# Relu and row mean on one core: tiles of 16 rows in 3 buffers instead of 8 rows in 6, and a last tile loaded in halving pieces

## The chip, the core and the metric

The kernel runs on one core of a Trainium2 chip. The metric is device time in microseconds (us), the median of several runs; lower is better. The engines that do work here are VectorE (DVE in the profile), ScalarE (ACT), and SyncE (SP), whose queue only issues transfers (DMAs). 16 DMA engines carry the transfers between the chip's main memory and the core's own memory. The core's own memory has 128 partitions, and a tile is a block of columns on all of them.

## The reference

```python
def setup_inputs():
    batch, seq, dim = 32, 512, 1024
    return {"x": np.random.randn(batch, seq, dim).astype(np.float32)}

def reference(x):
    relu_x = np.maximum(x, 0)
    return np.mean(relu_x, axis=-1).astype(np.float32)
```

Every one of the 16384 rows of 1024 floats is clipped at zero and averaged. 67.1 MB are read and 64 KB are written; there is one clip and one addition for each number.

## The kernel before, in words

The 16384 rows are dealt to the partitions: partition p holds the 128 neighbouring rows 128p to 128p+127, so that its input is one stretch of 512 KB. Below, "a row" is one row on every partition: 128 x 1024 floats, 512 KB.

The work goes over 16 tiles. A tile is 8 rows, which is 32 KB on each partition and 4 MB in all, and is loaded by one DMA from SP's queue (line 36). The pool named `in` has 6 buffers, so the first six loads are issued at once, and each later load waits on SP until the tile that had its buffer has been worked through.

The rows of a tile are shared out one by one. ScalarE takes the even rows (line 40): an activation with Relu, in place, whose accumulator gives the sum of the row. VectorE takes the odd rows (line 47): a maximum with zero, in place, again with an accumulator. Each accumulator is stored by a short instruction of its own behind the main one, which the profile lists as a READ_ACCUMULATOR. The sums go into one column for each row: `res_s` from ScalarE, `res_v` from VectorE.

Behind the last tile, line 56 (VectorE) scales the odd columns of `res_v` by 1/1024 into `res_s`, line 57 (ScalarE) scales the even columns of `res_s`, and line 58 stores `res_s`, 512 bytes on each partition, from SP's queue.

A framework sets the waits between the engines from what each instruction reads and writes. In the listings of the order, a wait such as DMAHW3 is a wait for the landing of a transfer (eight such counters are used in turn), DVE and Activation are waits for VectorE's and ScalarE's earlier work. Each engine runs its instructions in program order.

Of the kernel before, what the change touches and what calls it, by code (L numbers as in the profile page):

```python
# [1 line left out]

# [4 lines left out]


@with_exitstack  # L10
def kernel(
    ctx: ExitStack,
    tc: tile.TileContext,
    x: bass.AP,
    out: bass.AP,
):
    nc = tc.nc
    P = nc.NUM_PARTITIONS
    xf = x.flatten_outer_dims()
    R, D = xf.shape  # L20
    assert R % P == 0
    J = R // P
    xr = xf.rearrange("(p j) d -> p j d", p=P, j=J)
    outr = out.flatten().rearrange("(p j) -> p j", p=P, j=J)

    nb = 8
    assert J % nb == 0
    ntiles = J // nb

    with tc.tile_pool(name="in", bufs=6) as pool, tc.tile_pool(name="res", bufs=1) as rpool:  # L30
        res_s = rpool.tile([P, J], mybir.dt.float32)
        res_v = rpool.tile([P, J], mybir.dt.float32)
        for t in range(ntiles):
            j0 = t * nb
            xt = pool.tile([P, nb, D], mybir.dt.float32)
            nc.sync.dma_start(out=xt, in_=xr[:, j0:j0 + nb, :])  # L36
            for n in range(nb):
                j = j0 + n
                if j % 2 == 0:
                    nc.scalar.activation(  # L40
                        out=xt[:, n, :],
                        in_=xt[:, n, :],
                        func=mybir.ActivationFunctionType.Relu,
                        accum_out=res_s[:, j:j + 1],
                    )
                else:
                    nc.vector.tensor_scalar(  # L47
                        out=xt[:, n, :],
                        in0=xt[:, n, :],
                        scalar1=0.0,  # L50
                        scalar2=None,
                        op0=mybir.AluOpType.max,
                        op1=mybir.AluOpType.add,
                        accum_out=res_v[:, j:j + 1],
                    )
        nc.vector.tensor_scalar_mul(out=res_s[:, 1::2], in0=res_v[:, 1::2], scalar1=1.0 / D)  # L56
        nc.scalar.mul(out=res_s[:, 0::2], in_=res_s[:, 0::2], mul=1.0 / D)  # L57
        nc.sync.dma_start(out=outr, in_=res_s)


# [1 line left out]
_INS = ['x']  # L62
_OUTS = [((32, 512), 'float32')]


# [23 lines left out]
```

## Time and profile before

| what | value |
|---|---|
| time, median of 3 runs | 169.04 us (168.8 to 169.05) |
| span of the profiled execution, first to last instruction | 166.8 us |
| time outside the span, against that median | 2.2 us |
| VectorE busy | 74.5 us, 45% of the span |
| ScalarE busy | 69.8 us, 42% of the span |
| main memory read, mean over the span | 67.11 MB, 403 GB/s with the store |
| first and last tile, VectorE starts on it | 13.40 us and 159.42 us |
| store of the result issued | 164.37 us |

The span runs from the first to the last instruction on the core. The profiled execution has no separate device time of its own on record; the timed runs are 2.2 us above its span, which is what lies ahead of the first instruction and behind the last. "Busy" counts the time in which an engine runs instructions; waits are listed apart with the thing that ended them. The DMA share is the mean over the 16 DMA engines. A window counts a transfer's packet, with all its bytes and its whole duration, in the window in which it starts.

### The profile page before, as it was taken

How to read it: one execution, taken by the hardware profiler on the slowest of the kernel's cores; microseconds unless marked ns; L12 is line 12 of the kernel's file. 1: busy time of each engine (PE TensorE's matmuls, PEld its weight loads, DVE VectorE, ACT ScalarE, POOL GpSimd, SP SyncE). 2: the span in 40 equal slices, each digit the busy share in tenths (PEclk: the TensorE clock that was granted, in tenths of full speed). 3: DMA queues.
4: the chain of work that ended last, by engine and by line, in shares of the span. 5: the costliest groups of instructions: out<-in, count | busy, mean ns of one | idle time of the engine just before them, and what ended most of it. 6: DMA issues, size and time to landing. Idle time of an engine off the chain costs nothing.

```text
span 166.8 us, 353 instructions
## 1 busy us (share of the span) xinstructions
DVE 74.5 (45%) x129; ACT 69.8 (42%) x130; POOL 0.2 (0%) x4
## 2 busy tenths in 40 slices
DVE  0007346190734619073460907347090734609073
ACT  3007245180724518072450907246090724519073
POOL 0000000000000000000000000000000000000000
DMA  6999999999999999999999999999999999999700
GB/s 228 401 448 432 440 432 432 440 401 448 424 448 424 440 432 409 456 409 448 432 420 432 440 440 409 448 424 432 432 440 432 424 440 417 440 432 432 338 0 16
DMA packets 2450, 67.19 MB, mean 403 GB/s; under 512 B 272, under 2 KB 400, under 8 KB 400
## 3 DMA queue, kind: packets, MB, share of 16 engines
q1 hardware_dynamic: 2448, 67.18, 93.9%
q14 instruction: 2, 0.02, 0.0%
HBM read 67.11 MB, written 0.07 MB: 403 GB/s over the span
## 4 chain that ended last, share of the span: by engine, by line
DVE 34%; another core or an unknown queue 33%; DMA 29%; SPq 1%; issue 1%; DVEq 0%
DVE xt L47 33%; DMA xt<-in_x_dram 29%; SPq L36 1%; DVEq L47 0%; DVE res_s L56 0%
## 5 line engine op out<-in xcount | busy, mean ns | idle before, releaser
L47 DVE TENSOR_SCALAR_CACHE_REDUCE xt<-xt 128x1024 f32<-128x1024 f32 x64 | 74.2, 1216 | 89.7 <-DMA xt<-in_x_dram 89.7
L40 ACT ACTIVATE xt<-xt 128x1024 f32<-128x1024 f32 x64 | 66.8, 1044 | 93.4 <-DMA xt<-in_x_dram 93.4
L40 ACT ACTIVATION_READ_ACCUMULATOR xt<-xt 128x1 f32 x64 | 11.9, 187 | 0.0
L47 DVE DVE_READ_ACCUMULATOR xt<-xt 128x1 f32 x64 | 5.3, 83 | 0.0
L40 ACT ACT_TABLE_LOAD x1 | 1.3, 1283 | 0.7 <-PEq L73 0.7
L57 ACT ACTIVATE res_s<-res_s 128x64 f32<-128x64 f32 x1 | 0.3, 263 | 0.0
L56 DVE TENSOR_SCALAR res_s<-res_v 128x64 f32<-128x64 f32 x1 | 0.2, 196 | 0.0
L73 POOL MEMSET const-uint8-127<- 128x1 uint8 x1 | 0.1, 102 | 0.0
L73 POOL MEMSET const-bfloat16-1.0<- 128x1 bf16 x1 | 0.1, 101 | 0.0
L73 POOL MEMSET const-float32-0.0<- 128x1 f32 x1 | 0.1, 98 | 0.2 <-issue 0.2
L73 POOL MEMSET const-float32-1.0<- 128x1 f32 x1 | 0.1, 98 | 0.0
## 6 DMA issues: line engine op xcount, KB each, us to landing
xt<-in_x_dram SPq DMA_DIRECT2D x16, 4096.0 KB, 53.5
out_dram<-res_s SPq DMA_DIRECT2D x1, 64.0 KB, 1.6
```

The source lines that it names most:

```text
L36: nc.sync.dma_start(out=xt, in_=xr[:, j0:j0 + nb, :])
L40: nc.scalar.activation(out=xt[:, n, :], in_=xt[:, n, :], func=mybir.ActivationFunctionType.Relu, accum_out=res_s[:, j:j + 1],)
L47: nc.vector.tensor_scalar(out=xt[:, n, :], in0=xt[:, n, :], scalar1=0.0, scalar2=None, op0=mybir.AluOpType.max, op1=mybir.AluOpType.add, a ...
L56: nc.vector.tensor_scalar_mul(out=res_s[:, 1::2], in0=res_v[:, 1::2], scalar1=1.0 / D)
L57: nc.scalar.mul(out=res_s[:, 0::2], in_=res_s[:, 0::2], mul=1.0 / D)
L73: nc = _bacc.Bacc("TRN2", target_bir_lowering=False, num_devices=1)
```

## The change

The tile is 16 rows: 64 KB on each partition, 8 MB in all, in 3 buffers, so the memory for input stays the same. Seven such tiles are loaded whole. The eighth is loaded by seven DMAs into one buffer: 8, 4, 2 and 1 rows, and then the last row in columns of 512, 256 and 256. The rows are shared out as before up to row 13 of that tile. Row 14 is halved: ScalarE sums its first 512 columns, VectorE the rest, and VectorE adds the two. Of the last row, ScalarE sums the first 256 columns, VectorE the other three quarters one by one, with a small instruction that adds what is there before the last quarter. The means of the first 112 rows are written ahead of the last tile (`finish(0, j0)`), those of the next 14 ahead of row 14. The results now go to a tile `res` of their own.

```diff
-    nb = 8
-    assert J % nb == 0
-    ntiles = J // nb
+    NB = 16
+    BUFS = 3
+    full = J // NB - 1
 
-    with tc.tile_pool(name="in", bufs=6) as pool, tc.tile_pool(name="res", bufs=1) as rpool:
-        for t in range(ntiles):
-            j0 = t * nb
-            xt = pool.tile([P, nb, D], mybir.dt.float32)
-            nc.sync.dma_start(out=xt, in_=xr[:, j0:j0 + nb, :])
...
-        nc.vector.tensor_scalar_mul(out=res_s[:, 1::2], in0=res_v[:, 1::2], scalar1=1.0 / D)
-        nc.scalar.mul(out=res_s[:, 0::2], in_=res_s[:, 0::2], mul=1.0 / D)
-        nc.sync.dma_start(out=outr, in_=res_s)
+    row_pieces = []
+    left = NB
+    while left > 1:
+        row_pieces.append(left // 2)
+        left -= left // 2
+    col_pieces = [D // 2, D // 4, D // 4]
...
+    def rows(xt, lo, n, j0):
+        for k in range(lo, lo + n):
+            j = j0 + k
+            if j % 2:
+                dve_row(nc, xt[:, k, :], sum_v[:, j:j + 1])
+            else:
+                act_row(nc, xt[:, k, :], sum_a[:, j:j + 1])
+
+    def finish(lo, hi):
+        nc.vector.tensor_scalar_mul(out=res[:, lo + 1:hi:2], in0=sum_v[:, lo + 1:hi:2], scalar1=inv)
+        nc.scalar.mul(out=res[:, lo:hi:2], in_=sum_a[:, lo:hi:2], mul=inv)
+
+    for t in range(full):
+        j0 = t * NB
+        xt = in_pool.tile([P, NB, D], F32, name="xt")
+        nc.sync.dma_start(out=xt, in_=xr[:, j0:j0 + NB, :])
+        rows(xt, 0, NB, j0)
+
+    j0 = full * NB
+    xt = in_pool.tile([P, NB, D], F32, name="xt")
+    lo = 0
+    for n in row_pieces:
+        nc.sync.dma_start(out=xt[:, lo:lo + n, :], in_=xr[:, j0 + lo:j0 + lo + n, :])
+        lo += n
+    c = 0
+    for w in col_pieces:
+        nc.sync.dma_start(out=xt[:, lo, c:c + w], in_=xr[:, j0 + lo, c:c + w])
+        c += w
+
+    finish(0, j0)
+    lo = 0
+    for n in row_pieces[:-1]:
+        rows(xt, lo, n, j0)
+        lo += n
+    finish(j0, j0 + lo)
+
+    last = xt[:, NB - 1, :]
+    act_row(nc, xt[:, lo, :D // 2], part_a[:, 0:1])
+    dve_row(nc, xt[:, lo, D // 2:], part_v[:, 0:1])
+    act_row(nc, last[:, :D // 4], part_a[:, 1:2])
+    dve_row(nc, last[:, D // 4:D // 2], part_v[:, 1:2])
+    nc.vector.tensor_scalar(
+        out=res[:, J - 2:J - 1], in0=part_a[:, 0:1], scalar1=part_v[:, 0:1], scalar2=inv,
+        op0=ALU.add, op1=ALU.mult,
+    )
+    dve_row(nc, last[:, D // 2:3 * D // 4], part_v[:, 2:3])
+    nc.vector.tensor_scalar(
+        out=part_v[:, 1:2], in0=part_v[:, 1:2], scalar1=part_a[:, 1:2], scalar2=part_v[:, 2:3],
+        op0=ALU.add, op1=ALU.add,
+    )
+    dve_row(nc, last[:, 3 * D // 4:], part_v[:, 3:4])
+    nc.vector.tensor_scalar(
+        out=res[:, J - 1:J], in0=part_v[:, 3:4], scalar1=part_v[:, 1:2], scalar2=inv,
+        op0=ALU.add, op1=ALU.mult,
+    )
+    nc.sync.dma_start(out=outr, in_=res)
```

`act_row` and `dve_row` are the two instructions of before (an activation with Relu and an accumulator, a maximum with zero and an accumulator), now in functions: line 15 and line 20 of the changed kernel.

On SP's queue, the last five transfers of before, each but the store a whole tile:

```order
L36 DMA xt<-in_x_dram 128x8192 [waits DMAHW6_49,DVE_49,Activation_49]
L36 DMA xt<-in_x_dram 128x8192 [waits DMAHW7_49,DVE_49,Activation_49]
L36 DMA xt<-in_x_dram 128x8192 [waits DMAHW0_49,DVE_49,Activation_49]
L36 DMA xt<-in_x_dram 128x8192 [waits DMAHW1_49,DVE_49,Activation_49]
L58 DMA out_dram<-res_s 128x128 [waits DVE_49,Activation_49]
```

And SP's queue in the changed kernel, from the last whole tile on:

```order
L79 DMA xt<-in_x_dram 128x16384 [waits DMAHW3_49,DVE_49,Activation_49]
L86 DMA xt<-in_x_dram 128x8192 [waits DMAHW4_49,DVE_49,Activation_49]
L86 DMA xt<-in_x_dram 128x4096
L86 DMA xt<-in_x_dram 128x2048
L86 DMA xt<-in_x_dram 128x1024
L90 DMA xt<-in_x_dram 128x512
L90 DMA xt<-in_x_dram 128x256
L90 DMA xt<-in_x_dram 128x256 [waits DMAHW5_49]
L120 DMA out_dram<-res 128x128 [waits DMAHW6_49,DVE_49,Activation_49]
```

The last 8 MB come in seven transfers instead of two. The first piece waits for the buffer of the fifth whole tile, the five behind it wait for nothing, and the last one waits for the landing of the sixth whole tile.

On VectorE, the end of the program before: the last two tiles of four odd rows each, and the scaling.

```order
L47 TENSOR_SCALAR xt,res_v<-xt 128x1024 [waits DMAHW6_49,DVE_49,Activation_49]
L47 TENSOR_SCALAR xt,res_v<-xt 128x1024 x3
L47 TENSOR_SCALAR xt,res_v<-xt 128x1024 [waits DMAHW7_49,DVE_49,Activation_49]
L47 TENSOR_SCALAR xt,res_v<-xt 128x1024 x3
L56 TENSOR_SCALAR res_s<-res_v 128x64 [waits DVE_49]
```

And the end of VectorE's program in the changed kernel, from the piece of four rows on (`part_a` and `part_v` hold the partial sums of the last two rows):

```order
L20 TENSOR_SCALAR xt,sum_v<-xt 128x1024 [waits DMAHW0_49]
L20 TENSOR_SCALAR xt,sum_v<-xt 128x1024
L20 TENSOR_SCALAR xt,sum_v<-xt 128x1024 [waits DMAHW1_49]
L73 TENSOR_SCALAR res<-sum_v 128x7 [waits DVE_49]
L20 TENSOR_SCALAR xt,part_v<-xt 128x512 [waits DMAHW2_49]
L106 TENSOR_SCALAR res<-part_a,part_v 128x1 [waits DVE_49,Activation_49]
L20 TENSOR_SCALAR xt,part_v<-xt 128x256 [waits DMAHW3_49]
L20 TENSOR_SCALAR xt,part_v<-xt 128x256 [waits DMAHW4_49]
L111 TENSOR_SCALAR part_v<-part_v,part_a 128x1 [waits DVE_49,Activation_49]
L20 TENSOR_SCALAR xt,part_v<-xt 128x256 [waits DMAHW5_49]
L116 TENSOR_SCALAR res<-part_v 128x1 [waits DVE_49]
```

Behind the landing of the last transfer stand one row of 256 columns and one instruction of one column, where four rows and one instruction of 64 columns stood. The addition for row 14 (line 106) comes ahead of the first column piece of the last row, though it stands behind it in the code.

More of the change, by code (lines that the diff above doesn't have):

```diff
@@ L7, with act_row, dve_row @@
 from concourse._compat import with_exitstack
+F32 = mybir.dt.float32
+ALU = mybir.AluOpType
+RELU = mybir.ActivationFunctionType.Relu
+def act_row(nc, src, acc):
+    nc.scalar.activation(out=src, in_=src, func=RELU, accum_out=acc)
+def dve_row(nc, src, acc):
+    nc.vector.tensor_scalar(
+        out=src, in0=src, scalar1=0.0, scalar2=None,
+        op0=ALU.max, op1=ALU.add, accum_out=acc,
+    )
 @with_exitstack
@@ L22 @@
     J = R // P
+    inv = 1.0 / D
     xr = xf.rearrange("(p j) d -> p j d", p=P, j=J)
     outr = out.flatten().rearrange("(p j) -> p j", p=P, j=J)
-    nb = 8
-    assert J % nb == 0
-    ntiles = J // nb
-    with tc.tile_pool(name="in", bufs=6) as pool, tc.tile_pool(name="res", bufs=1) as rpool:
-        res_s = rpool.tile([P, J], mybir.dt.float32)
-        res_v = rpool.tile([P, J], mybir.dt.float32)
-        for t in range(ntiles):
-            j0 = t * nb
-            xt = pool.tile([P, nb, D], mybir.dt.float32)
[L36 to L58, printed above, removed]
@@ new lines @@
+    NB = 16
[7 more added lines that the diff above has]
+    col_pieces = [D // 2, D // 4, D // 4]
+    in_pool = ctx.enter_context(tc.tile_pool(name="in", bufs=BUFS))
+    res_pool = ctx.enter_context(tc.tile_pool(name="res", bufs=1))
+    sum_a = res_pool.tile([P, J], F32)
+    sum_v = res_pool.tile([P, J], F32)
+    res = res_pool.tile([P, J], F32)
+    part_a = res_pool.tile([P, 2], F32)
@@ new lines @@
+    part_v = res_pool.tile([P, 4], F32)
+    def rows(xt, lo, n, j0):
[13 more added lines that the diff above has]
+        rows(xt, 0, NB, j0)
@@ L62 @@
+    dve_row(nc, last[:, 3 * D // 4:], part_v[:, 3:4])
+    nc.vector.tensor_scalar(
+        out=res[:, J - 1:J], in0=part_v[:, 3:4], scalar1=part_v[:, 1:2], scalar2=inv,
+        op0=ALU.add, op1=ALU.mult,
+    )
+    nc.sync.dma_start(out=outr, in_=res)
 _INS = ['x']
```

## The prediction

> **What bounds the kernel now.** I read the page first (busy shares, DMA line, costliest groups), then the waits, then windows one tile long, then the timeline of the end. The page:
>
> ```profile
> span 166.8 us, 353 instructions
> DVE 74.5 (45%) x129; ACT 69.8 (42%) x130; POOL 0.2 (0%) x4
> DMA  6999999999999999999999999999999999999700
> ...
> DMA packets 2450, 67.19 MB, mean 403 GB/s; under 512 B 272, under 2 KB 400, under 8 KB 400
> ...
> L47 DVE TENSOR_SCALAR_CACHE_REDUCE xt<-xt 128x1024 f32<-128x1024 f32 x64 | 74.2, 1216 | 89.7 <-DMA xt<-in_x_dram 89.7
> L40 ACT ACTIVATE xt<-xt 128x1024 f32<-128x1024 f32 x64 | 66.8, 1044 | 93.4 <-DMA xt<-in_x_dram 93.4
> L40 ACT ACTIVATION_READ_ACCUMULATOR xt<-xt 128x1 f32 x64 | 11.9, 187 | 0.0
> L47 DVE DVE_READ_ACCUMULATOR xt<-xt 128x1 f32 x64 | 5.3, 83 | 0.0
> ...
> L57 ACT ACTIVATE res_s<-res_s 128x64 f32<-128x64 f32 x1 | 0.3, 263 | 0.0
> L56 DVE TENSOR_SCALAR res_s<-res_v 128x64 f32<-128x64 f32 x1 | 0.2, 196 | 0.0
> ...
> xt<-in_x_dram SPq DMA_DIRECT2D x16, 4096.0 KB, 53.5
> out_dram<-res_s SPq DMA_DIRECT2D x1, 64.0 KB, 1.6
> ```
>
> Neither engine is half busy, and all that they wait for is the input. The DMA engines are full until two or three slices before the end. Tile by tile (columns: window, length, VectorE, ScalarE, GpSimd, clock, DMA share, GB/s):
>
> ```profile
> 61.97:71.81 9.84, 4.65 (x9) 4.31 (x9) 0.00 (x0) 1.00 1.00 433
> 71.81:81.51 9.70, 4.64 (x9) 4.26 (x9) 0.00 (x0) 1.00 1.01 432
> 81.51:91.45 9.94, 4.64 (x9) 4.26 (x9) 0.00 (x0) 1.00 1.00 430
> 130.30:140.02 9.72, 4.65 (x9) 4.27 (x9) 0.00 (x0) 1.00 1.00 432
> 140.02:149.74 9.72, 4.66 (x9) 4.28 (x9) 0.00 (x0) 1.00 1.00 432
> ```
>
> A tile lands every 9.7 us and takes 4.65 us of work. The DMA share is 1.00 across the joint from one transfer to the next: 4.19 MB / 9.71 us is 432 GB/s, the rate inside the window, so nothing is lost at a joint. So the stream sets the time until its last byte, and the end is what VectorE does behind it:
>
> ```profile
> 13.40 1.22 DVE L47 TENSOR_SCALAR_CACHE_REDUCE xt<-xt 128x1024 f32<-128x1024 f32 x1 [13.40 <-DMA xt<-in_x_dram]
> ...
> 149.72 1.22 DVE L47 TENSOR_SCALAR_CACHE_REDUCE xt<-xt 128x1024 f32<-128x1024 f32 x1 [5.07 <-DMA xt<-in_x_dram]
> ...
> 159.38 1.06 ACT L40 ACTIVATE xt<-xt 128x1024 f32<-128x1024 f32 x1 [5.44 <-DMA xt<-in_x_dram]
> 159.42 1.22 DVE L47 TENSOR_SCALAR_CACHE_REDUCE xt<-xt 128x1024 f32<-128x1024 f32 x1 [5.06 <-DMA xt<-in_x_dram]
> 160.57 0.08 DVE L47 DVE_READ_ACCUMULATOR xt<-xt 128x1 f32 x1
> 160.57 1.22 DVE L47 TENSOR_SCALAR_CACHE_REDUCE xt<-xt 128x1024 f32<-128x1024 f32 x1
> ...
> 163.99 0.08 DVE L47 DVE_READ_ACCUMULATOR xt<-xt 128x1 f32 x1
> 164.10 0.20 DVE L56 TENSOR_SCALAR res_s<-res_v 128x64 f32<-128x64 f32 x1
> ```
>
> The last tile is seen at 159.42 and VectorE ends at 164.30: 4.88 us of tail. A row starts 1.15 us after the one ahead of it, and lasts 1.22 with its accumulator read. From 164.30 to the span's end are 2.5 us for the store, which the change leaves as it is:
>
> ```profile
> 164.37 0.35 SPq L58 DMA_DIRECT2D out_dram<-res_s  x1
> ```
>
> **The change, part by part.** *Buffers.* A tile of 16 rows lands every 19.4 us (twice 9.7) and needs about 9.2 us of VectorE (8 rows by 1.14, and 0.08). The fourth load is issued when the first tile has been worked through, near 32.3 (8 rows land at 13.40, 16 at 13.40 + 9.7 = 23.1, and 9.2 behind that), when two loads of 8 MB are still under way until 23.1 + 38.8 = 61.9: 29 us to spare, and the same for each load behind it. SP's waits now:
>
> ```profile
> SPq L36 <- DVE xt L47: 98.3, 10, 14.0
> ```
>
> SP already waits 98.3 us in ten waits with nothing lost at the joints; all that stands behind such a wait on SP are later loads. The six added issues (0.35 us by the store's row, 0.4 by the first loads) lie near 110 us, when the sixth and seventh tile are queued. The last piece also waits for the sixth tile, which lands near 120, almost 40 us before that piece is due. Cost of all this: nothing; cover: the queued loads. Without the cover a late issue would cost its own lateness.
>
> *Packets.* No row shows a packet over 32 KB. In the full windows above a DMA engine moves 432/16 = 27.0 GB/s, so a packet of 32 KB takes 1.214 us. The smallest data packets are the store's 128 of 512 bytes, and they come with 16 of a few bytes for the counter:
>
> ```profile
> 164.90:165.90 1.00, 0.00 (x0) 0.00 (x0) 0.00 (x0) 1.00 0.23 66
> 157.50:158.00 0.50, 0.00 (x0) 0.00 (x0) 0.00 (x0) 1.00 0.16 66
> ```
>
> 0.23 x 1 us x 16 / 128 = 28.8 ns for each. A line through both gives, as an estimate, 9.9 ns for a packet and 36.8 ns for a KB. The page's 2450 packets are 16 tiles x 128 of 32 KB, the 128 of the store, and small ones, so a DMA engine moves 128 of 32 KB; the change has 7 x 8 of 64 KB and 7 x 8 in the pieces, 112: 16 x 9.9 ns = 0.16 us less. Bounds: a gain of 0.55 us if 64 KB packets save their half (56 x 9.9 ns) and the pieces pay nothing more; for the loss there is no row. A 64 KB packet slower by p costs 56p, and the whole gain below is gone at p = 64 ns, 2.6% of 2.43 us. I take 0.1 us of gain, as the rate of 432 holds at 32 KB and the packets cost only by their count in these two rows.
>
> *The tail.* With the joints free, the piece of 8 rows ends where the tile before last does now, at 149.72, and 9.70/8 = 1.21 us pass for a row. So VectorE can see: 4 rows at 154.57, 2 rows at 157.00, row 14 at 158.21, the columns at 158.82, 159.12 and 159.42. Durations by the line through 1216 ns (1024 columns) and 196 ns (64): 1.0625 ns a column, so 672 ns for 512, 400 for 256, 135 for 7, 130 for one. An instruction that waits for VectorE's own last result starts 0.03 later (163.99 + 0.08 to 164.10). VectorE's chain:
>
> The last whole tile lands where a window ends above, at 140.02, is done at 149.2, and its scaling (56 columns, 0.19) lies at 149.4: in time. 4 odd rows end at 154.36, 2 at 156.93, each just ahead of the next piece. Row 13: 157.00 to 158.22. Scaling of 7: to 158.39. Half of row 14: 158.41 to 159.08. Its addition: to 159.24. First columns: 159.25 to 159.65. Second: start 0.08 ahead of that end, as the rows do, to 159.97. Addition: to 160.13. Last columns: to 160.54. Last addition: to **160.70**.
>
> So the last columns are there at 159.42 and VectorE comes to them at 160.14. The landing is hidden by the chain from row 13 on, with 0.7 us to spare; a landing-bound end would be 159.42 + 0.40 + 0.16 = 159.98. ScalarE is a near tie: 8 x 1.04 a tile keeps it ahead; row 12 from 156.96 (it starts 0.04 ahead of VectorE) to 158.11, scaling of 7 (0.22) to 158.36, half of row 14 (1044 − 512 x 0.81 = 628 ns, and 0.09 of read) to 159.10, when VectorE asks for it at 159.11. If it comes later, the chain moves by as much. The addends with a wait are bounded by 83 ns (accumulator read) and 196 ns (64 columns), so the three additions by −0.14 and +0.20 us together. And a wait for a DMA costs VectorE a little of its own, as the chain of waits has it for the last tile:
>
> ```profile
> 159.28 0.03 issue
> 159.31 0.05 DVEq L47
> 159.36 0.06 issue
> 159.42 4.66 DVE xt L47 x8
> ```
>
> The landing times above hold this 0.14 where VectorE waits. At the four waits behind which it finds the data there, I put 0.03 each, and 0.1 in all; the bounds are nothing and 4 x 0.14 = 0.56.
>
> The Trainium skill ("VectorE: DVE Perf Modes", on the extra latency of SBUF-source instructions) has a fixed cost of about 150 cycles in each instruction, 156 ns, where my line has 128 to 130. By the page the tail would end 0.17 us later; no run here has yet shown a row of 256 columns.
>
> *Sum.* 164.30 − 160.70 = 3.60 us less of tail, 0.1 less of stream, and 0.1 against it for the added waits: the span goes from 166.8 to 163.2. The 2.2 us outside it stay. Against the median of 169.04, which I take for this execution's own time, that is **165.4 us**, 2.1% faster.
>
> **The rivals.**
>
> *A: the landing sets the end, and comes earlier.* Packets of 64 KB gain 0.55, the two windows of 9.84 and 9.94 lose their excess of 0.35, and the small instructions are at their low bound. For it: those two windows. Against it: the chain on VectorE from row 13 on is as long as before, and only what moves row 13 counts. Time: 165.4 − 0.55 − 0.14 = 164.7; with the 0.35, 164.4.
>
> *B: the small column pieces come in late.* The store of 64 KB needs 1.6 us from issue to landing, though its packets are moved in a part of that. If each of the three column pieces (256, 128, 128 KB) took 1.6 us behind the one ahead, the last would be seen at 158.21 + 4.8 = 163.01, and VectorE would end at 163.57: 2.87 us later, 168.3 us. Against it: the joints at full share. In between, up to 0.7 us of lateness costs nothing, since VectorE comes at 160.14.
>
> *C, slower than before: each piece pays for its start and its landing in line.* All six added joints cost 1.6 us: the last columns are seen at 159.42 + 9.6 = 169.0, VectorE ends at 169.6, 5.3 us later than now: 174.3 us. It decides from (164.30 − 0.56 − 159.42)/6 = 0.72 us a joint. For it: the 1.6 us. Against it: fifteen joints of 4 MB transfers without a gap, and the pieces are queued 40 us ahead. The Trainium skill ("DMA: Bandwidth & Descriptors", under the anatomy of one DMA and the measured bandwidths) gives some 2.0 us fixed for each DMA and asks for 1 MiB or more in each. Taken in line at its figure, the last landing is 12 us later and the time 176.7 us; the windows above speak against taking it in line.
>
> *D: 64 KB packets are cut in two, or are slower.* Cut in two, the packets are those of before and the forecast stands within 0.5 us. Slower by 64 ns each, the time is 169.0; nothing in the rows shows that, and nothing shows the opposite.
>
> **How the numbers follow.** Forecast 0.70, its own range 164.9 to 166.0 (the bounds on the additions, the waits, the ScalarE tie). A 0.12, B 0.09, C 0.04, D at or above the old time 0.05. The range takes in A and the near part of B (half a microsecond past the cover): 164.4 to 166.4. A measurement of this kernel can tell about 0.2%, 0.34 us, from no change. Faster: 0.70 + 0.12 + 0.08 of B = 0.90; the same: 0.01 of B and 0.03 of D; slower: 0.04 + 0.02.
>
> **What would show it.** Windows of 19.4 us at 432 GB/s show packets and buffers right; a window above 19.9 shows D. VectorE's start on row 13 near 157.0 shows the joints free. On the last columns VectorE should show no wait for a DMA, and start near 160.1; idle time there for a DMA of over 0.3 us shows B. A wait of the addition of row 14 for ScalarE shows the tie lost. VectorE's end should be near 160.7 and the span near 163.2. A span over 165 makes the prediction wrong, and then the landing times of the pieces say which step fell.

## The result, and the profile after

The changed kernel takes 164.86 us (median of 4 runs, 164.74 to 164.88) beside 168.95 us before (4 runs, 168.80 to 169.05): a ratio of 0.9765, 95% interval 0.9751 to 0.9779, 2.3% faster. The forecast was 165.4 us in a range of 164.4 to 166.4. The span of the profiled execution went from 166.8 to 163.1 us, where the prediction had 163.2.

The page of the changed kernel:

```profile
span 163.1 us, 351 instructions
DVE 75.4 (46%) x139; ACT 69.4 (43%) x133; POOL 0.2 (0%) x4
...
DMA packets 2162, 67.19 MB, mean 412 GB/s; under 512 B 240, under 2 KB 624, under 8 KB 880
...
L20 DVE TENSOR_SCALAR_CACHE_REDUCE xt<-xt 128x1024 f32<-128x1024 f32 (+1 forms) x67 | 74.4, 1172 | 84.9 <-DMA xt<-in_x_dram 84.8
```

Both engines are as busy as before, and still wait only for the input. The packets fell from 2450 to 2162 (896 for the whole tiles, 896 for the pieces, 128 of the store and 242 small ones), so the 16 rows do come as one packet of 64 KB on each partition: rival D's first half (packets cut in two) is out. Windows of the change, each between VectorE's starts on two whole tiles that follow one another (window, length, VectorE, ScalarE, GpSimd, clock, DMA share, GB/s):

```profile
42.50:61.90 19.40, 9.21 (x17) 8.43 (x17) 0.00 (x0) 1.00 1.00 432
61.90:81.40 19.50, 9.23 (x17) 8.48 (x17) 0.00 (x0) 1.00 0.99 430
100.90:120.30 19.40, 9.22 (x17) 8.47 (x17) 0.00 (x0) 1.00 1.00 432
```

The stream is full, with 9.2 us of work under each 19.4 us of loading. The timeline of the end, VectorE and what it meets (start, duration):

```profile
149.32 1.22 DVE L20 TENSOR_SCALAR_CACHE_REDUCE xt<-xt 128x1024 f32<-128x1024 f32 x1 [0.24 <-DMA xt<-in_x_dram]
...
156.62 1.22 DVE L20 TENSOR_SCALAR_CACHE_REDUCE xt<-xt 128x1024 f32<-128x1024 f32 x1
...
157.88 0.17 DVE L73 TENSOR_SCALAR res<-sum_v 128x7 f32<-128x7 f32 x1
157.91 0.63 ACT L15 ACTIVATE xt<-xt 128x512 f32<-128x512 f32 x1
157.96 0.68 DVE L20 TENSOR_SCALAR_CACHE_REDUCE xt<-xt 128x512 f32<-128x512 f32 x1
...
158.75 0.21 DVE L106 TENSOR_SCALAR res<-part_a,part_v 128x1 f32<-128x1 f32 x1
...
158.88 0.41 DVE L20 TENSOR_SCALAR_CACHE_REDUCE xt<-xt 128x256 f32<-128x256 f32 x1
...
159.22 0.42 DVE L20 TENSOR_SCALAR_CACHE_REDUCE xt<-xt 128x256 f32<-128x256 f32 x1
...
159.75 0.27 DVE L111 TENSOR_SCALAR part_v<-part_v,part_a 128x1 f32<-128x1 f32 x1
159.94 0.41 DVE L20 TENSOR_SCALAR_CACHE_REDUCE xt<-xt 128x256 f32<-128x256 f32 x1
...
160.39 0.21 DVE L116 TENSOR_SCALAR res<-part_v 128x1 f32<-128x1 f32 x1
```

Row 13 starts at 156.62, where the prediction had 157.00. VectorE never waits for a DMA behind it (no bracket behind the rows), and ends at 160.60, where the prediction had 160.70. So from row 13 on VectorE needs 3.98 us, not 3.70. By the counters in the trace, the piece with row 13 landed at 156.59, row 14 at 157.89, and the columns at 158.5, 158.9 and 159.2. VectorE comes to the last columns at 159.94, 0.75 us behind their landing.

### The profile page after: what moved, and what is told of

Same layout as the page of the kernel before. It is cut to its first block, busy times and chain, and to the rows that moved or that the text cites. A ratio compares the mean times of both kernels' runs of the same rounds, so it can differ in the third digit from the quotient of the medians.

```text
span 163.1 us, 351 instructions
## 1 busy us (share of the span) xinstructions
DVE 75.4 (46%) x139; ACT 69.4 (43%) x133; POOL 0.2 (0%) x4
## 2 busy tenths in 40 slices
DMA packets 2162, 67.19 MB, mean 412 GB/s; under 512 B 240, under 2 KB 624, under 8 KB 880
## 4 chain that ended last, share of the span: by engine, by line
DMA 83%; DVE 14%; SPq 1%; issue 0%; DVEq 0%
DMA xt<-in_x_dram 83%; DVE xt L20 13%; SPq L86 0%; SPq L79 0%; DVE part_v L111 0%; DVE res L116 0%; DVE res L106 0%; DVE res L73 0%; DVEq L20 0%; DVEq L111 0%; DVEq L106 0%
## 5 line engine op out<-in xcount | busy, mean ns | idle before, releaser
L20 DVE TENSOR_SCALAR_CACHE_REDUCE xt<-xt 128x1024 f32<-128x1024 f32 (+1 forms) x67 | 74.4, 1172 | 84.9 <-DMA xt<-in_x_dram 84.8
L15 ACT ACTIVATE xt<-xt 128x1024 f32<-128x1024 f32 (+1 forms) x65 | 66.7, 1027 | 88.9 <-DMA xt<-in_x_dram 88.9
L74 ACT ACTIVATE res<-sum_a 128x56 f32<-128x56 f32 (+1 forms) x2 | 0.5, 232 | 0.1
```

The costliest lines, as they stand in the source:

```text
L15: nc.scalar.activation(out=src, in_=src, func=RELU, accum_out=acc)
L20: nc.vector.tensor_scalar(out=src, in0=src, scalar1=0.0, scalar2=None, op0=ALU.max, op1=ALU.add, accum_out=acc,)
L74: nc.scalar.mul(out=res[:, lo:hi:2], in_=sum_a[:, lo:hi:2], mul=inv)
```

## The experiments

Each kernel was timed beside the kernel before on one chip, whose median there was 168.78, 168.82 and 168.80 us in the three groups (1 to 4, 5 to 8, 9 to 12). The theory was: the stream moves 67.1 MB at a rate that only its packet count changes; VectorE's chain from row 13 on, and not the last landing, sets the end.

One thing that no edit was meant to change moves the end by up to 0.2 us. In every profile the store lands 1.54 to 1.57 us behind its issue. But the last work of SyncE is to check the counters of the transfers one after another, some 0.06 us apart, and the store's counter is one of them. Which one it is follows from the number of loads, since the eight counters are used in turn. The checks from the store's own counter on come behind its landing, so they lengthen the span:

| checks behind the store's landing | kernels, with their loads | landing to the span's end, us |
|---|---|---|
| 2 | before (16) | 0.85 |
| 3 | the change and experiments 3, 7, 8, 11, 12 (14), 2 (9) | 0.88 to 0.92 |
| 4 | 1 (21), 6 (13) | 0.94, 0.96 |
| 5 | 4 (36), 5 and 10 (12) | 1.00, 1.01 |
| 6 | 9 (11) | 1.06 |

None of the expectations below knew of it. Where two kernels differ in it, 0.06 us for each check is taken off before their times are read.

### 1. The tail alone, on tiles of 8 rows

```diff
-    NB = 16
-    BUFS = 3
+    NB = 8
+    BUFS = 6
```

> The tail of the change on tiles of 8 rows (32 KB a partition) in 6 buffers: 15 whole tiles, then 4, 2, 1 rows and the three column pieces. Against the change, 120 packets of 32 KB and 48 smaller ones on a DMA engine instead of 56 of 64 KB and 56 smaller: 56 more. Theory (a packet costs about 9 ns whatever its size, and the larger packets brought the stream forward by it): 56 x 9 ns = 0.5 us more than the change, 165.35 us. Rival (the packet size does nothing, the stream's 0.4 us came from elsewhere in the change, for instance from the fewer waits of SP): 164.9 us.

Measured: 165.57 us (165.49 to 165.78), ratio 0.9808 (0.9796 to 0.9821). The mark on the same chip is experiment 3, which is as fast as the change: 165.01. So tiles of 8 rows cost 0.56 us, of which 0.06 is one more check, and the rival is out. VectorE's row 13:

```profile
157.17 1.22 DVE L20 TENSOR_SCALAR_CACHE_REDUCE xt<-xt 128x1024 f32<-128x1024 f32 x1
```

It is 0.55 later than in the change (and 0.49 later than in experiment 3, where it starts at 156.68), and 0.50 us by 56 packets is 8.9 ns a packet (with the counters of seven more transfers in it). The tail is worth 168.78 − 165.57 = 3.2 us by itself.

### 2. The large tiles alone

```diff
-    row_pieces = []
-    left = NB
-    while left > 1:
-        row_pieces.append(left // 2)
-        left -= left // 2
-    col_pieces = [D // 2, D // 4, D // 4]
+    row_pieces = [8, 8]
...
-    finish(0, j0)
...
+    rows(xt, 0, NB, j0)
+    finish(0, J)
```

> Tiles of 16 rows in 3 buffers, the last one loaded as 8 + 8 rows, with the end of the kernel before (four odd rows and the scaling behind the last landing). Theory (packets bring 0.4 us, the halving pieces all the rest): 168.5 us, VectorE's start on the last 8 rows near 159.0 and its end near 163.9 us in the span. Rival (large tiles alone bring nothing): 168.95 us. A second rival (large tiles cost, and the pieces pay for it): over 169.2 us.

Measured: 168.38 us (12 runs, 168.05 to 169.00), ratio 0.9975 (0.9966 to 0.9985): 0.40 us less, as the theory has it, and 0.46 without the one check more. The timeline of the last tile:

```profile
159.15 1.22 DVE L20 TENSOR_SCALAR_CACHE_REDUCE xt<-xt 128x1024 f32<-128x1024 f32 x1 [4.94 <-DMA xt<-in_x_dram]
...
163.82 0.20 DVE L66 TENSOR_SCALAR res<-sum_v 128x64 f32<-128x64 f32 x1
```

The start was 159.42 before, 0.27 later in this pair of executions, and the 4.87 us behind it are those of before. Not all of the 0.27 is the stream's. The tile before landed at 159.28 and VectorE started 0.14 behind that, since its first row waits for three counters (the order listing of before), two of them in an instruction of its own ahead of the row. Here the piece landed at 159.12 and the row, which has one wait, started 0.02 behind. Without these 0.12 the times leave 0.34 us for the packets, 6 ns for each of 56 fewer.

The two halves of the change, 0.4 and 3.2 us, add up to 3.6 of the 3.8 us that experiment 3 shows for both on this chip.

### 3. Two buffers

```diff
-    BUFS = 3
+    BUFS = 2
```

> The change with 2 buffers instead of 3. Theory (a load is needed in the queue only while the one ahead runs, and it is issued 9.2 us after a landing with 19.4 us of the next tile to go, so 10 us early): no change, 164.9 us within 0.2. Rival (the queue has to hold two waiting loads, or the deeper queue hides something at the joint): 165.9 us or more, with windows of 19.4 us below 430 GB/s.

Measured: 165.01 us (164.93 to 165.12), ratio 0.9774 (0.9761 to 0.9786). The change repeated on other chips gave 164.99 and 164.89: no difference, as the theory has it. SP's waits, and the last whole tile:

```profile
SPq L79 <- DVE xt L20: 107.1, 5, 30.8
```

```profile
139.69 1.22 DVE L20 TENSOR_SCALAR_CACHE_REDUCE xt<-xt 128x1024 f32<-128x1024 f32 x1 [10.15 <-DMA xt<-in_x_dram]
```

SP waits 107.1 us for buffers where the change waits 87.4, and the tile still lands within 0.05 us of the change's 139.64. The third buffer is not needed.

### 4. Tiles of 4 rows

```diff
-    NB = 16
-    BUFS = 3
+    NB = 4
+    BUFS = 12
```

> The tail of the change on tiles of 4 rows (16 KB a partition) in 12 buffers: 31 whole tiles, then 2, 1 rows and the column pieces, 248 + 40 packets on a DMA engine, 176 more than in the change. Theory (9 ns a packet): 1.6 us more than the change, 166.45 us. Rival (32 KB is past a knee below which packets cost much more, or joints of smaller transfers cost): 167.5 us or more. Other rival (packet size does nothing): 164.9 us.

Measured: 166.68 us (166.64 to 166.69), ratio 0.9872 (0.9859 to 0.9884): 1.67 us over experiment 3, 1.55 without the two checks more, for 176 packets: 8.8 ns each with the counters of 22 more transfers. A window of the full stream, and row 13:

```profile
80.00:100.00 20.00, 9.47 (x16) 8.76 (x16) 0.00 (x0) 1.00 1.01 428
```

```profile
158.30 1.21 DVE L20 TENSOR_SCALAR_CACHE_REDUCE xt<-xt 128x1024 f32<-128x1024 f32 x1
```

The DMA engines stay full and only the rate falls, to 428 GB/s. There is no knee from 64 KB down to 16 KB a packet, just the count. The packets themselves say the same. In the trace of the change there are packets of every size from 512 bytes (the store) to 64 KB, each twice the one below, and their median durations are 27, 46, 84, 159, 309, 611, 1213 and 2418 ns. All of them are 8 ns and 37.7 ns a KB, within 3 ns.

### 5. The last row in one transfer

```diff
-    col_pieces = [D // 2, D // 4, D // 4]
+    col_pieces = [D]
```

> The change, but the last row comes in one transfer of 512 KB instead of columns of 512, 256 and 256; all instructions of the engines stay. Theory (VectorE's chain from row 13 on sets the end, with 0.8 us of cover over the last landing): the whole row is seen at 159.15 by VectorE, which wants its first columns at 158.88 in the change, so only 0.3 us are added, 165.15 us beside 164.86. Rival (the last landing sets the end): three transfers become one, the last byte comes 0.1 to 0.2 us earlier, and the time falls to 164.7. Second rival (each column piece saves its own share of waiting, as the halving suggests): the first 512 columns are 0.6 us later, 165.5 us.

Measured: 165.09 us (165.03 to 165.15), beside 164.99 for the change in the same group (experiment 8). Theory's direction, but only 0.1 us of it, and the trace says why:

```profile
156.58 1.22 DVE L20 TENSOR_SCALAR_CACHE_REDUCE xt<-xt 128x1024 f32<-128x1024 f32 x1
...
159.09 0.42 DVE L20 TENSOR_SCALAR_CACHE_REDUCE xt<-xt 128x256 f32<-128x256 f32 x1 [0.16 <-DMA xt<-in_x_dram]
...
160.11 0.27 DVE L111 TENSOR_SCALAR part_v<-part_v,part_a 128x1 f32<-128x1 f32 x1
...
160.42 0.21 DVE L116 TENSOR_SCALAR res<-part_v 128x1 f32<-128x1 f32 x1
```

VectorE does wait now, 0.16 us, and comes to the columns 0.25 later behind row 13 than in the change (2.51 against 2.26), near the 0.3 of the theory. But with one transfer to wait for, the framework put the addition of line 111 behind the last quarter of the row, where its operand is long there and its 0.1 of wait is gone. From row 13 on that makes 4.05 us against 3.98. So the column pieces and the order that comes with them are worth 0.07 us; what the pieces would be worth in the other order, no run tells. The two checks more would add 0.12 to the time; that only 0.10 is measured in all lies within what executions of one kernel differ by (experiment 8).

### 6 and 7. A shorter chain on VectorE, and once more with quarters

In both, ScalarE scales as it sums and takes the first half of the last row, VectorE takes row 14 whole, GpSimd scales what is left, and one addition remains on VectorE. In 7 the second half of the last row comes and is summed in two quarters. The diff of 7:

```diff
-    nc.scalar.activation(out=src, in_=src, func=RELU, accum_out=acc)
+    nc.scalar.activation(out=src, in_=src, func=RELU, scale=1.0 / 1024, accum_out=acc)
...
-    finish(j0, j0 + lo)
+    dve_row(nc, xt[:, lo, :], sum_v[:, J - 2:J - 1])
...
+    act_row(nc, last[:, :D // 2], part_a[:, 0:1])
+    nc.gpsimd.tensor_scalar_mul(out=res[:, j0 + 1:J - 2:2], in0=sum_v[:, j0 + 1:J - 2:2], scalar1=inv)
+    nc.gpsimd.tensor_scalar_mul(out=res[:, J - 2:J - 1], in0=sum_v[:, J - 2:J - 1], scalar1=inv)
+    dve_row(nc, last[:, D // 2:3 * D // 4], part_v[:, 0:1])
+    nc.scalar.activation(out=part_a[:, 1:2], in_=part_v[:, 0:1], func=mybir.ActivationFunctionType.Identity,
+                         scale=inv, bias=part_a[:, 0:1])
+    dve_row(nc, last[:, 3 * D // 4:], part_v[:, 1:2])
+    nc.vector.tensor_scalar(
+        out=res[:, J - 1:J], in0=part_v[:, 1:2], scalar1=inv, scalar2=part_a[:, 1:2],
+        op0=ALU.mult, op1=ALU.add,
+    )
```

> The change with less on VectorE behind row 13: ScalarE scales by 1/1024 in its activation and needs no scaling of its own; VectorE takes row 14 whole and then one half of the last row, ScalarE the other half; the column pieces are two of 512; GpSimd scales the odd columns behind row 111 and row 14; one addition is left. The stream's end stays. Theory (VectorE's chain sets the end): row 14 from 157.84, done at 158.98, then the last 512 columns at their landing, 159.1, with the addition behind them at 159.85 to 160.1, so 0.5 us less than the change, 164.35 us, and now a short wait of VectorE for the last landing. Rival (the last landing, not the chain, sets the end of the change): with 0.68 us of work behind the last landing instead of 0.41, no gain or 0.3 us more, 164.9 to 165.1.

> As the kernel with the short chain, but the second half of the last row comes and is summed in two quarters, and ScalarE adds the first three quarters while VectorE sums the last. Theory: the last quarter can start at 159.3, the addition ends at 159.95: 164.25 us, 0.1 less than with halves. Rival (an added handover between VectorE and ScalarE costs more than the quarter saves): 164.5 us.

Measured: 164.81 us (164.73 to 164.92) for 6, a gain of 0.18 where 0.5 was expected; 164.63 us (164.49 to 164.90) for 7, a gain of 0.36 where 0.6 was expected; the change in the same group is at 164.99. VectorE in 6, from row 13 on:

```profile
156.92 1.22 DVE L20 TENSOR_SCALAR_CACHE_REDUCE xt<-xt 128x1024 f32<-128x1024 f32 x1
...
158.21 1.22 DVE L20 TENSOR_SCALAR_CACHE_REDUCE xt<-xt 128x1024 f32<-128x1024 f32 x1
...
159.47 0.69 DVE L20 TENSOR_SCALAR_CACHE_REDUCE xt<-xt 128x512 f32<-128x512 f32 x1
...
160.28 0.21 DVE L102 TENSOR_SCALAR res<-part_v,part_a 128x1 f32<-128x1 f32 x1
```

From row 13 on these are 3.57 us, 0.41 less than in the change. VectorE is now so early that it meets the landings. Row 14 starts 1.29 behind row 13, at its own landing (158.18), where the expectation had 1.22. On the last columns VectorE is free at 159.43, and the chain of work that ended last puts its start on their landing at 159.45:

```profile
112.83 46.62 DMA xt<-in_x_dram
159.45 0.02 issue
159.47 0.70 DVE xt L20 x2
```

So the short wait that was expected is there, but it is a tie. Work behind the last landing went up and the time went down: the landing did not set the end of the change. Of the 0.41 us, one check more takes 0.06; the rest of the way to the measured 0.18 lies within what executions differ by. In 7:

```profile
156.69 1.22 DVE L20 TENSOR_SCALAR_CACHE_REDUCE xt<-xt 128x1024 f32<-128x1024 f32 x1
...
159.64 0.29 ACT L102 ACTIVATE part_a<-part_v,part_a 128x1 f32<-128x1 f32 x1 [0.30 <-DVE xt L20]
...
159.99 0.21 DVE L105 TENSOR_SCALAR res<-part_v,part_a 128x1 f32<-128x1 f32 x1
```

3.51 us from row 13 on, with as many checks as in the change. ScalarE's addition ends at 159.93, in time: VectorE's last addition starts 0.11 behind VectorE's own read (159.88), as the one of 6 does (160.17 to 160.28), so no cost of the handover shows.

### 8. The change again

No edit.

> The change once more, on the chip of the three beside it, so that differences of 0.2 us can be read: 164.85 us. If it is over 0.2 us from that, the chips differ by as much and only runs of one chip are compared.

Measured: 164.99 us (164.86 to 165.26), ratio 0.9772 (0.9759 to 0.9785). The profiled execution among these is the one of 165.26, and its row 13 starts at 157.02 with the same 3.98 us behind it. So executions of one kernel differ by some 0.4 us in where the stream ends, and lengths from row 13 on tell more than single times.

### 9. The last two rows in one piece, nothing halved

```diff
...
+    row_pieces = [8, 4, 2, 2]
...
+    for n in row_pieces:
+        rows(xt, lo, n, j0)
+        lo += n
+    finish(j0, J)
```

> The change without its finest pieces: the last tile in 8, 4, 2 and 2 rows, no row halved and no columns; each engine sums its row of the last piece and scales its column of eight. Theory (the landing of the last bytes and the work behind it, against VectorE's chain of 4.0 us in the change): the last two rows are seen 2.49 us behind row 13's piece, 1.22 us of row and 0.2 of scaling follow: 3.9 us from row 13 on beside 3.98, so the same as the change within 0.2 us, 164.9. Rival (each halving brings its share, half of the last landing's work): the last landing has 1.42 us behind it where the change has about 0.6: 165.7 us.

Measured: 165.30 us (165.15 to 165.62), beside 164.89 for the change in its group (experiment 12): 0.4 us more, between the theory and the rival. From row 13 on VectorE did as the theory has it:

```profile
156.78 1.22 DVE L20 TENSOR_SCALAR_CACHE_REDUCE xt<-xt 128x1024 f32<-128x1024 f32 x1
...
159.23 1.22 DVE L20 TENSOR_SCALAR_CACHE_REDUCE xt<-xt 128x1024 f32<-128x1024 f32 x1 [1.22 <-DMA xt<-in_x_dram]
...
160.49 0.17 DVE L66 TENSOR_SCALAR res<-sum_v 128x8 f32<-128x8 f32 x1
```

3.88 us, against 3.98 for the change. But from VectorE's end to the span's end pass 163.4 − 160.66 = 2.7 us, where the change has 2.5 (163.1 − 160.60). The store is not the reason: it lands 1.57 us behind its issue, against 1.55. With 11 loads it has the counter that is checked first, so six checks come behind its landing instead of three, 0.19 us. That and the shorter chain make 0.1 us more than the change; the rest of the 0.4 lies in where the stream ends (row 13 starts 0.12 later than in the profile of experiment 12) and in the differences between executions.

### 10. One row more in one piece, halved between the engines

Pieces of 8, 4, 2, 1 and 1 rows; ScalarE scales as in 6 and takes row 14.

```diff
-    col_pieces = [D // 2, D // 4, D // 4]
+    col_pieces = [D]
...
-    finish(j0, j0 + lo)
+    finish(j0, J - 2)
+    act_row(nc, xt[:, lo, :], res[:, J - 2:J - 1])
...
+    act_row(nc, last[:, :D // 2], part_a[:, 0:1])
+    dve_row(nc, last[:, D // 2:], part_v[:, 0:1])
+    nc.vector.tensor_scalar(
+        out=res[:, J - 1:J], in0=part_v[:, 0:1], scalar1=inv, scalar2=part_a[:, 0:1],
+        op0=ALU.mult, op1=ALU.add,
+    )
```

> Pieces of 8, 4, 2, 1 and 1 rows; ScalarE scales in its activation and takes row 14 whole; VectorE scales its odd rows while it waits; the last row comes whole and is halved between the two, with one addition. Theory: the last row is seen 2.5 us behind row 13's piece, 0.68 of half row, 0.12 of wait and 0.21 of addition follow: 3.5 us from row 13 on, 0.5 us less than the change, 164.4 us, and VectorE waits for the last landing. Rival (the columns of the change are needed to hide the landing): 165.1 us.

Measured: 164.78 us (164.55 to 164.99), 0.1 us below the change of its group, where 0.5 was expected.

```profile
156.66 1.22 DVE L20 TENSOR_SCALAR_CACHE_REDUCE xt<-xt 128x1024 f32<-128x1024 f32 x1
...
159.16 0.69 DVE L20 TENSOR_SCALAR_CACHE_REDUCE xt<-xt 128x512 f32<-128x512 f32 x1 [1.06 <-DMA xt<-in_x_dram]
...
159.96 0.21 DVE L101 TENSOR_SCALAR res<-part_v,part_a 128x1 f32<-128x1 f32 x1
```

VectorE idles 1.06 us for the landing and still ends 3.51 us behind row 13, as 7 does with hardly a wait. So the 0.5 us are there in the chain. Two checks more take back 0.12 of it (162.8 − 160.17 = 2.63 us from VectorE's end to the span's). The profiled execution, at 164.55 us, is 0.36 below the one of experiment 12 (164.91), as these two make it. The median is not, because two of the four runs are at 164.94 and 164.99; that is the scatter of experiment 8.

### 11 and 12. Quarters again, and the change a third time

> The kernel with the short chain and quarters once more, beside the others on one chip: 0.3 to 0.4 us below the change. If it is not below it, the first reading was scatter between runs.

> The change once more, as the mark for the three beside it: 164.9 us within 0.2.

Measured: 164.65 us (164.55 to 164.76) for 11, ratio to the kernel before 0.9753 (0.9740 to 0.9766); 164.89 us (164.87 to 164.95) for 12, ratio 0.9767 (0.9753 to 0.9780). The kernel with quarters is below the change in both groups, by 0.36 and 0.24 us, where the chain gives 0.47; no run of it in the second group reaches the lowest of the change. The intervals of the two ratios overlap, so the gain of 0.2% over the change is likely, not certain.

## Why the prediction was right, point by point

**The bound.** Right: the stream of 67.1 MB sets the time until its last packets, and the gain is at the end. The tail alone gave 3.2 of the 3.8 us.

**Buffers and issues.** Right, at no cost: even two buffers change nothing. The last piece's wait for the sixth tile is done at 120, as the prediction had it.

**Packets.** The mechanism was right, and the term was too small: 0.1 us taken, 0.34 and 0.50 measured (experiments 2 and 1, without the checks). The price of 9.9 ns a packet was a little high: 6 to 9 ns from the times, 8 from the packets' durations. (The slope beside it has a slip: a line through 28.8 and 1214 ns has 37.6 ns a KB, not 36.8; nothing was worked out from it.) What failed is the balance of 128 against 112 packets: the small packets of the columns and of row 14 lie behind row 13's landing, under VectorE's chain. Only what comes ahead of row 13's data counts: 7 x 8 of 64 KB and 3 x 8 in the pieces, 80, against 126 rows' worth of packets before, 46 x 9.9 ns = 0.45 us. At 8 ns it is 0.37. The landings go with it: row 13's piece landed 0.27 us ahead of the prediction's time (157.00 less the 0.14 that it holds, against 156.59), the last columns only 0.10. The bound of 0.55 contained it.

**The tail.** The form was right: VectorE's chain, not the landing, sets the end (5, 6, 8). Its length was 0.28 us too short, or 0.18 with the 0.1 that the sum holds for added waits. Groups of the changed kernel, shapes apart (mean ns behind the busy time):

```profile
L20 DVE TENSOR_SCALAR_CACHE_REDUCE xt<-xt 128x256 f32<-128x256 f32 x3 | 1.2, 412 | 0.0
L20 DVE TENSOR_SCALAR_CACHE_REDUCE xt<-xt 128x512 f32<-128x512 f32 x1 | 0.7, 679 | 0.0
...
L111 DVE TENSOR_SCALAR part_v<-part_v,part_a 128x1 f32<-128x1 f32 x1 | 0.3, 273 | 0.1
...
L106 DVE TENSOR_SCALAR res<-part_a,part_v 128x1 f32<-128x1 f32 x1 | 0.2, 214 | 0.1
L116 DVE TENSOR_SCALAR res<-part_v 128x1 f32<-128x1 f32 x1 | 0.2, 214 | 0.0
...
L73 DVE TENSOR_SCALAR res<-sum_v 128x56 f32<-128x56 f32 x1 | 0.2, 195 | 0.0
L73 DVE TENSOR_SCALAR res<-sum_v 128x7 f32<-128x7 f32 x1 | 0.2, 174 | 0.0
```

The rows were right within 3% (672 and 400 forecast). The additions were not: 214, 273 and 214 ns, outside the bound of 83 to 196, where 130 was taken. And the two that wait for ScalarE too start 0.11 us behind the read ahead of them, not 0.03, because the second wait has an instruction of its own (DVEq):

```profile
158.66 0.03 issue
158.68 0.02 DVEq L106
158.71 0.05 issue
158.75 0.21 DVE res L106
```

In the chain the addition of line 111, with its wait, cost 0.13 us more than forecast, the last one 0.09. The line of the prediction ran through two different instructions, a sum over 1024 columns and a scaling of 64. Each has a line of its own: the sum 143 ns and 1.05 ns a column (679 and 1216), the scaling 171 ns and 0.43 ns a column between 7 and 56 columns (174 and 195), with 154 ns for one column in experiment 4. Beside these 154, an addition with one operand for each partition read from a tile takes 214, and with two 273. The second of them goes with 59 ns, since both additions have two operations; whether the first 60 are the operand's or the second operation's, no run takes apart. The Trainium skill ("VectorE: DVE Perf Modes", on the extra latency of SBUF-source instructions) has about 150 cycles fixed, 156 ns as an estimate at the clock in its table: nearer to the 143 and 154 to 171 of these traces than the prediction's 128 to 130.

**ScalarE's near tie.** Held: ScalarE's read ended at 158.64, together with VectorE's own, and the addition of row 14 starts 0.11 behind. That is no wait for ScalarE, since the addition of line 111 starts 0.11 behind VectorE's read as well (159.64 to 159.75), and ScalarE's part of that had ended at 159.06.

**The sum.** The stream's error (0.38 us too late at row 13: 0.27 at the landing and 0.11 because the row has one wait and starts 0.02 to 0.03 behind it, not 0.14) and the tail's (0.28 too short) nearly cancel, and the span came out at 163.1 for 163.2. That is luck in part: in experiment 8 the same kernel's row 13 starts at 157.02, as forecast, and its span is 163.5. The time was off by 0.5 us for another reason: the 2.2 us around the span. The changed kernel's profiled execution took 164.88 us with a span of 163.1, so 1.8 us lie outside; and runs of the kernel before, listed later with their spans, have 166.9 for 168.71 and 167.0 for 168.78. The profiled execution of before, with its 166.8, thus took about 168.6, below every run of its own group (168.80 to 169.05), and the median of 169.04 was not its time. With 1.8 us the forecast would have been 165.0.

**The rivals.** A (earlier landing): its part on packets came true within its bound; the end was not the landing's. B and C: no column piece was waited for. The columns of 256, 128 and 128 KB landed 0.6, 0.35 and 0.3 us behind the piece ahead of each, and in 10 the last 1 MB is seen 2.5 us behind the piece ahead of it, which is 1.05 MB / 2.5 us = 420 GB/s. The Trainium skill ("DMA: Bandwidth & Descriptors", anatomy of one DMA) gives its fixed 2 us for a DMA that GpSimd issues; these are issued by SyncE. Here no such time is paid in line by queued pieces down to 128 KB: the measurement decides. D: packets of 64 KB come whole and are no slower.

## What to carry to other kernels

Where a stream sets the time, the tail behind its last bytes is what a kernel can still win: cut the last load so that the compute behind the last landing is short, but only until the engine that follows is no longer waiting. From there on the chain of one engine is what to shorten: with whole rows and nothing halved (experiment 9) VectorE was done 0.1 us sooner behind row 13 than with the finer pieces of the change, and with a shorter chain (7 and 10) 0.5 us sooner. Cost a short instruction from a row of the same kind, and take the time outside the span from a run whose span is known. Before a difference of 0.1 us is explained, look at what each kernel does behind its last store.

## What was not expected of the hardware

A transfer's packet costs 8 ns beside 37.7 ns a KB, whatever its size from 512 bytes to 64 KB, and that is all that the tile size does to a full stream (428 GB/s at 16 KB, 430 to 432 at 64 KB). And the number of loads in a program moves its end: from the store's landing to the end of the span pass 0.85 us with 16 loads and 1.06 with 11, because SyncE checks the counters of the transfers one by one, and the place of the store's counter in that row follows from the number of loads. A wait for several counters costs an engine time of its own even when all are there: VectorE started 0.02 us behind a landing with one wait, and 0.14 with three.
